# Buffers of the up projections' second pass and the modulation's transfers in a two-block transformer kernel

## The chip, the cores and the metric

The kernel runs as one program on one core of a Trainium2 chip. The metric is the time of one execution on the device in microseconds (us); several executions are timed and their median is given. A profiled execution, recorded by the hardware profiler, gives the trace from which all rows below are taken. TensorE (PE) multiplies, VectorE (DVE), ScalarE (ACT) and GpSimd (POOL) work on tiles in SBUF and PSUM, and SyncE (SP) issues most of the DMA transfers.

## The reference

Two transformer blocks on a sequence of 1024 tokens of width 1024, in float32. The first has a gated delta rule group and a latent attention group, the second a short convolution, stick-breaking attention and a modulation of six rows computed from a conditioning vector c. Both end in a feed-forward network of width 4096 with a squared ReLU. The change lies in the up projections of these two networks and in the modulation:

```python
# first block
h = rms_norm(x, ffn_pre_norm[l])
f = jnp.square(jax.nn.relu(h @ w_up[l])) @ w_down[l]
x = x + rms_norm(f, ffn_post_norm[l])
...
# second block
mod = c @ w_ada[l] + b_ada[l]
sh1, sc1, gt1, sh2, sc2, gt2 = jnp.split(mod, N_MOD, axis=-1)
...
h2 = modulate(rms_norm_2(x, g_pre_mlp[l]), sh2, sc2)
ff = jnp.square(jax.nn.relu(h2 @ w_mlp_in[l])) @ w_mlp_out[l]
x = x + gt2[:, None, :] * rms_norm_2(ff, g_post_mlp[l])
```

## The kernel before

The order of instructions on each engine is fixed when the program is built: a scheduler places them by its own estimate of times, under the waits that tiles and their buffers impose. Each engine then runs its instructions in that order, and SP issues its DMAs in its order. A named tile with `*n` in `TAGS` has n buffers used in turn; a new tile of that name waits until the readers and writers of the one n before are done.

All matrix products split each float32 operand into a high and a low part (`hi`, `lo`) and take three matmuls for one. The up projections, `ffn_up`, use a Strassen-like scheme in which 2x2 blocks need seven products. It is called twice by `up_stage`: in stage 1 with `w_up` (second pass from about 745 to 1010 us) and in stage 2 with `w_mlp_in_2` (second pass from about 2210 to 2470 us). A first pass makes two products per chunk of 256 columns and writes them to `fx_dr` in DRAM. The second pass runs over the 16 chunks c and makes the other five products, each 12 matmuls of 128x128 by 128x512, into PSUM tiles of which six may be in use (`mm_tile`).

For chunk c the second pass needs:

- the raw weights, 1 MB, from `load` (L1065). They go in turn into `w_raw` (even c) and into quarter 0 of a large tile, `hq` (odd c). The load of c+2 waits until the last reader of the raw weights of c is done.
- `fx` and `f00` from `load_x` (L1072), 256 KB each, both from `fx_dr`. The tile called `f00` here becomes `f11` in the loop (L1135) and is read by GpSimd at the end of the chunk; the trace calls it `f`.
- four sums and differences of quarters of the raw weights, from `weight_sums` (L1080) on VectorE; they go in turn into quarters 1 and 2 of `hq`. The fifth operand is a quarter of the raw weights themselves, called a22.
- for each of the five operands a split into high and low part (`parts`): two copies on ScalarE (L1093 and L1095) and a subtraction on VectorE (L1096). The split for a22 is the one whose L1096 reads `w_raw` or quarter 0 directly.

As products come, VectorE combines them (L1134, L1135, L1140, L1143, L1145, L1150, L1153), ScalarE applies ReLU and square (L1055, L1056), and GpSimd makes five more sums per chunk in tiles called `fs` (L1158) and stores them, 256 KB each (L1046). L1134 comes once per chunk.

In stage 1 the modulation runs beside this as `side`: it loads `w_ada_2` in slabs (L1275) into quarter 3 of `hq`, multiplies and adds them on VectorE (L1288, L1290), reduces each accumulated row on TensorE, copies it on ScalarE (L1246) and stores it with SP (L1247). The rest of the modulation runs in the same way beside the second block's convolution, with its own tiles `ada_raw`.

After the second pass, `ffn_down` loads weights (L1182) and the stored tiles (L1170).

Of the kernel before, what the change touches and what calls it, by code (L numbers as in the profile page):

```python
# [8 lines left out]
F32 = mybir.dt.float32  # L9
# [8 lines left out]
P = 128  # L18
# [15 lines left out]
TAGS = {  # L34
# [5 lines left out]
}  # L40
# [25 lines left out]
def tile_two_blocks(ctx: ExitStack, tc: tile.TileContext, I, out):  # L66
    nc = tc.nc
    PE, ACT, DVE, POOL, SP = nc.tensor, nc.scalar, nc.vector, nc.gpsimd, nc.sync
# [86 lines left out]
    mod_raw = scratch("mod_raw", (6, D))  # L155
# [94 lines left out]
    def col(r):  # L250
        return vec[:, r:r + 1]
# [790 lines left out]
    def ffn_up(hq, w_up, fl, fp, first, side):  # L1042
# [30 lines left out]

        def weight_sums(c):
            (a11, a21), (a12, a22) = ([raws[c][:, h, i] for i in range(2)] for h in range(2))
            t = fp.tile([P, 4, 4, P], F32, name="fws") if c == 0 else hq.tile(1 + c % 2, [P, 4, 4, P], F32)
            s1, s2, s3, s4 = (t[:, n] for n in range(4))
            for o, y, z, op in ((s1, a21, a22, ALU.add), (s2, s1, a11, ALU.subtract), (s3, a11, a21, ALU.subtract),
                                (s4, a12, s2, ALU.subtract)):
                DVE.tensor_tensor(out=o, in0=y, in1=z, op=op)  # L1080
            sums[c] = s2, s3, s1, a22, s4
# [16 lines left out]
        with tc.high_priority(offset=100):  # L1098
            for c in range(NC):
# [8 lines left out]
                for i, b in enumerate(("b11", "b21")):  # L1108
                    acc = product([t[:, 8 * (c % 2) + 4 * i:8 * (c % 2) + 4 * i + 4] for t in w], b)
# [8 lines left out]
        for c in range(NC):  # L1118
# [6 lines left out]
            x, f11 = xs.pop(c)  # L1125
# [29 lines left out]
            for i, y, z, o in ((0, f11, f22, ALU.add), (4, f11, f12, ALU.add), (6, f12, f22, ALU.subtract),  # L1155
                               (1, f21, f22, ALU.add), (5, f21, f11, ALU.subtract)):
                t = fp.tile([P, 512], F32, name="fs")
# [84 lines left out]
    def modulation_sum(i, acc, pool):  # L1242
        row = pool.tile([P, 512], F32, name="fs")[0:1, :]
        p = mm_tile()
        PE.matmul(p[0:1, :], ones[:, 0:1], acc, start=True, stop=True)
        ACT.copy(row, p[0:1, :])  # L1246
        SP.dma_start(mod_raw[i // 2:i // 2 + 1, (i % 2) * 512:(i % 2) * 512 + 512], row)  # L1247

    def modulation_columns(pool, m0, m1):

# [16 lines left out]
    def modulation(pool, m0, m1, new_raw, m):  # L1267

        n = 8 // m

        def load(j):
            if j < 2 * m1 * n:
                i, q = divmod(j, n)
                raw = new_raw()
                SP.dma_start(raw, I["w_ada_2"][0][m * P * q:m * P * q + m * P, 512 * i:512 * i + 512]  # L1275
                             .rearrange("(k p) n -> p k n", p=P))
                return raw

        raw, acc = load(2 * m0 * n), None
        yield  # L1280
        for i in range(2 * m0, 2 * m1):
            if acc is not None:
                modulation_sum(i - 1, acc, pool)
            acc = pool.tile([P, 512], F32, name="ada_acc")
            for k in range(8):
                r = raw[:, k % m, :]
                if k == 0:
                    DVE.tensor_scalar(acc, r, col(R_C), None, ALU.mult)  # L1288
                else:
                    DVE.scalar_tensor_tensor(out=acc, in0=r, scalar=col(R_C + k), in1=acc, op0=ALU.mult, op1=ALU.add)  # L1290
                if k % m == m - 1:
                    raw = load(n * i + k // m + 1)
                if k % 2:
                    yield
        modulation_sum(2 * m1 - 1, acc, pool)
        modulation_columns(pool, m0, m1)
# [264 lines left out]
    with ExitStack():  # L1561
        with banks(mm=6, tr=2):
            rows = {}

            def gains1(ep):
                for nm, v in (("gpost", "mix_post_norm"), ("grow", "ffn_pre_norm")):
                    rows[nm] = ep.tile([P, D], F32, name=nm)
                    bcast_row(rows[nm], I[v][0], D)

            def side1(fp, hq):  # L1570
                g = modulation(fp, 0, 2, lambda: hq.tile(3, [P, 4, 512], F32), 4)

                def step(c):
                    next(g, None)
                    if c == 15:
                        for _ in g:
                            pass

                return step

            mx1 = ExitStack()
            mxp = stage(mx1, "mx", 4, side="right")
            up_stage(1, I["w_out"][0], mix_dr, mxp, mx1, I["w_up"][0], lambda t, y, ep, put: epilogue(
                t, y, rows["gpost"], ep, I["x"][0], x_dr[0], lambda t, xt, xn, junk: norm_to_hT(
                    t, xt, xn, junk, None, None, row=rows["grow"], tmp_pool=ep, put=put), spare=False),
                "gpost grow xt*2 yg htt", gains1, side1)
            htx = ExitStack()
            edge(htx, "edge")
            h = new_hT(stage(htx, "hT", 1, side="right"))
            with sbuf("dp", 1, tags=TAGS["dp"]) as dp:  # L1590
                with sbuf("yf", 1, side="right") as yp, sbuf("ep", 1, side="right", tags="gpost xt*2 junk yg hmod*2") as ep:
                    y = yp.tile([P, NT, D], F32, name="y")
                    gf = ep.tile([P, D], F32, name="gpost")
                    bcast_row(gf, I["ffn_post_norm"][0], D)
                    first = ffn_down(I["w_down"][0], y, dp, lambda t: epilogue(
                        t, y[:, t, :], gf, ep, x_dr[0], x_dr[1],
                        lambda t, xt, xn, junk: norm_to_hT(t, xt, xn, junk, h[0], h[1], gain=amod[:, 0:8], bias=mod[:, 0:8], tmp_pool=ep)),
                        lambda i: w_cols(w_in2, (1024, 512)[i], 256))
            with sbuf("pb", 2) as pb, sbuf("pm", 1, tags="ada_acc*2 ada_raw*3 fs") as pm:
                side = modulation(pm, 2, 6, lambda: pm.tile([P, 2, 512], F32, name="ada_raw"), 2)  # L1600
                block2_conv_qkv(h, w_in2, pb, first, side)
                for _ in side:
                    pass
        with sbuf("so", 2) as so:
            with sbuf("pg", 2) as pg, sbuf("sp", 2, tags=TAGS["sp"]) as sp, banks(mm=2, sc=2, tr=2, po=2):
                for _ in stick_breaking(sp, so):
                    pass
                for _ in gates2(h, w_in2, pg):
                    pass
            htx.close()  # L1610
            late.enter_context(banks(mm=6, tr=2))
            mx2 = ExitStack()
            mxp2 = mx2.enter_context(sbuf("mx2", 4, side="right"))
            with sbuf("mg", 2) as mg:
                for half in range(2):
                    for _ in merge(half, mg):
                        pass
# [44 lines left out]
```

## Time and profile before

| | us |
|---|---|
| runs | 2832.03, 2825.65, 2827.81 |
| median of the runs | 2827.81 |
| profiled execution | 2816.81 |
| its span in the trace | 2815.0 |
| TensorE busy | 2648.2 (94%) |
| VectorE busy | 1920.3 (68%) |
| ScalarE busy | 1406.8 (50%) |
| GpSimd busy | 833.6 (30%) |

The busy shares are averages over stages with different limits. What a change in the second passes is worth has to be read from their stretches: how busy TensorE is there, what VectorE waits for, and in which order loads are issued and used.

### The profile page before, as it was taken

What the parts mean: (1) busy time and instruction counts of PE and PEld (TensorE: products, weight loads), DVE (VectorE), ACT (ScalarE), POOL (GpSimd) and SP (SyncE); (2) the same over time, 40 slices, a digit from 0 to 9 for tenths busy, and PEclk for the clock granted to TensorE, in tenths of its full rate; (3) what the DMA queues carried; (4) which work ended last, traced back from release to release, by engine and by line L of the source; (5) the groups of instructions that cost most, each with busy time, mean ns of one, the idle gap of its engine ahead of it and who ended that gap; (6) DMA issues with size and microseconds to landing.
All of it is one profiled execution on the core that took longest, in us unless ns stands there. A gap on an engine that the chain in (4) does not pass through costs nothing.

```text
span 2815.0 us, 39760 instructions
## 1 busy us (share of the span) xinstructions
PE 2648.2 (94%) x13801; PEld 2233.5 (79%) x13801; DVE 1920.3 (68%) x3518; ACT 1406.8 (50%) x2592; POOL 833.6 (30%) x840
## 2 busy tenths in 40 slices
PE   7999999999998889999999999999999998889996
PEld 7788889998777768777887788887798787668785
DVE  7678789858687765577755358686568575565666
ACT  5544666546665544354521246564267565543342
POOL 1242353200165562324100022111200165553413
PEclk9999999999999999999999999999999999999998
DMA  4286576446767677777664645334756666687785
GB/s 131 80 292 198 160 209 178 115 161 214 238 233 237 236 284 239 256 242 257 206 205 140 212 144 175 105 116 153 249 177 221 208 220 204 204 280 252 268 285 182
DMA packets 390207, 574.83 MB, mean 204 GB/s; under 512 B 39939, under 2 KB 224362, under 8 KB 390006
## 3 DMA queue, kind: packets, MB, share of 16 engines
q1 hardware_dynamic: 358774, 496.78, 55.1%
q0 software_dynamic: 12800, 41.95, 3.8%
q10 hardware_dynamic: 18432, 33.56, 3.2%
q8 instruction: 109, 1.79, 0.3%
q14 instruction: 92, 0.75, 0.1%
HBM read 417.21 MB, written 154.98 MB: 203 GB/s over the span
## 4 chain that ended last, share of the span: by engine, by line
PE 26%; DMA 17%; DVE 10%; POOL 6%; ACT 4%; issue 3%; SPq 1%; POOLq 0%; DVEq 0%; ACTq 0%
PE mm L173 22%; DMA dwr<-in_w_mlp_out 3%; DVE w_lo L179 3%; DMA w_raw<-in_w_down 3%; DMA f<-fx_dr 2%; POOL fs L1158 2%; POOL dwr L1186 2%; POOL w_raw L1186 1%; ACT w_hi L178 1%; DMA dwr<-in_w_down 1%; PE po L909 1%; DVE w_lo L209 1%; DMA w_raw<-in_w_mlp_out 1%; DMA w_raw<-in_w_mlp_in 1%; PE tr L901 1%
## 5 line engine op out<-in xcount | busy, mean ns | idle before, releaser
L173 PE MATMUL mm<-w_hi,df 128*128 128x512 f32 x1792 | 559.9, 393 | 11.8 <-DVE df L179 3.3
L173 PE MATMUL mm<-hq_t,w_hi 128*128 128x512 f32 x1280 | 410.4, 403 | 50.8 <-DVE fu L1150 23.0
L173 PEld LDWEIGHTS mm<-w_hi,df 128*128 128x128 f32 x1792 | 339.2, 190 | 86.5 <-DVE df L179 3.8
L173 PE MATMUL mm<-w_lo,df 128*128 128x512 f32 x896 | 353.2, 394 | 18.5 <-DVE w_lo L179 18.5
L173 PEld LDWEIGHTS mm<-hq_t,w_hi 128*128 128x128 f32 x1280 | 245.1, 194 | 117.3 <-issue 33.2
L173 PE MATMUL mm<-h_hi,w_hi 128*128 128x512 f32 x736 | 290.9, 395 | 0.0
L173 PE MATMUL mm<-h_lo,w_hi 128*128 128x512 f32 x736 | 289.4, 393 | 0.0
L173 PE MATMUL mm<-h_hi,w_lo 128*128 128x512 f32 x736 | 289.0, 393 | 0.0
L173 PE MATMUL mm<-hq_t,w_lo 128*128 128x512 f32 x640 | 253.5, 398 | 0.0
L209 DVE TENSOR_TENSOR w_lo<-w_raw,w_hi 128x1024 fp32r<-128x1024 f32 (+1 forms) x146 | 182.5, 1273 | 103.1 <-ACT w_hi L203 102.7
L203 ACT CAST w_hi<-w_raw 128x1024 fp32r<-128x1024 f32 (+1 forms) x146 | 147.0, 1049 | 166.9 <-PE mm L173 58.3
L173 PEld LDWEIGHTS mm<-w_lo,df 128*128 128x128 f32 x896 | 170.0, 190 | 59.0 <-DVE w_lo L179 24.1
L179 DVE TENSOR_TENSOR df<-dfr,df 128x1024 fp32r<-128x1024 f32 x112 | 157.9, 1422 | 77.4 <-ACT df L178 77.4
L1186 POOL TENSOR_TENSOR dwr<-dwr 128x1024 f32<-128x1024 f32 x40 | 101.2, 2530 | 320.0 <-DMA dwr<-in_w_mlp_out 183.1
L173 PE MATMUL mm<-w_hi,mixT 128*128 128x256 f32 x1024 | 183.7, 281 | 4.1 <-ACT w_hi L203 1.7
L179 DVE TENSOR_TENSOR w_lo<-dwr,w_hi 128x1024 fp32r<-128x1024 f32 x56 | 107.5, 1920 | 102.7 <-ACT w_hi L178 102.2
L178 ACT CAST df<-dfr 128x1024 fp32r<-128x1024 f32 x112 | 115.8, 1050 | 104.6 <-PE mm L173 62.9
L173 PEld LDWEIGHTS mm<-h_hi,w_hi 128*128 128x128 f32 x736 | 138.3, 188 | 34.0 <-issue 2.8
L173 PEld LDWEIGHTS mm<-w_hi,mixT 128*128 128x128 f32 x1024 | 156.7, 188 | 6.0 <-ACT w_hi L203 3.7
L1158 POOL TENSOR_TENSOR fs<-f,f 128x512 f32<-128x512 f32 x32 | 42.8, 1338 | 397.0 <-ACT f L1056 396.8
L173 PEld LDWEIGHTS mm<-h_hi,w_lo 128*128 128x128 f32 x736 | 138.3, 188 | 27.3
L173 PE MATMUL mm<-hq,w_hi 128*128 128x512 f32 x512 | 159.5, 392 | 0.0
(420 smaller groups left out, 6227.5 us busy)
## 6 DMA issues: line engine op xcount, KB each, us to landing
dfr<-fs SPq DMA_DIRECT2D x112, 512.0 KB
fs<-fs POOLq DMA_DIRECT2D x160, 256.0 KB, 5.3
w_raw<-in_w_in SPq DMA_DIRECT2D x32, 1024.0 KB
dwr<-in_w_down SPq DMA_DIRECT2D x48, 512.0 KB
w_raw<-in_w_down SPq DMA_DIRECT2D x48, 512.0 KB
dwr<-in_w_mlp_out SPq DMA_DIRECT2D x48, 512.0 KB
w_raw<-in_w_mlp_out SPq DMA_DIRECT2D x48, 512.0 KB
w_raw<-in_w_out SPq DMA_DIRECT2D x16, 1024.0 KB
```

The costliest lines, as they stand in the source:

```text
L173: PE.matmul(ps, l, r, start=first and n == 0, stop=final and n == last)
L178: ACT.copy(hi, src)
L179: DVE.tensor_tensor(out=lo, in0=src, in1=r32(hi), op=ALU.subtract)
L203: ins = ACT.copy(wh[:, step * i:step * i + step], raw[:, step * i:step * i + step])
L209: DVE.tensor_tensor(out=wl[:, c], in0=raw[:, c], in1=r32(wh[:, c]), op=ALU.subtract)
L901: PE.transpose(pt[:, 256 * j + P * i:256 * j + P * i + P], prob[i][:, ks], ident)
L909: PE.matmul(po[:, d:], vb if j else va, t[:, 256 * j:256 * j + 256 - d], start=n == 0 and m == 0, stop=n == len(groups) - 1 and m == 3)
L1158: POOL.tensor_tensor(out=t, in0=y, in1=z, op=o)
L1186: POOL.tensor_tensor(out=a, in0=a, in1=b, op=ALU.subtract if sub else ALU.add)
```

## The change

Five edits. The sums of all chunks but the first go into one quarter of `hq` (quarter 1) where two were used in turn. `fx` gets three buffers for two, `f00` four for two, `fs` four for seven. The modulation's slabs in stage 1 use quarters 2 and 3 in turn where quarter 3 alone was used, and each slab is loaded one slab earlier, in the convolution stage too. The modulation's row is stored by ScalarE's DMA queue where it was SP's. Line numbers from L1275 on are larger by two after the change.

```diff
--- before.py
+++ after.py
@@ -34,7 +34,7 @@
 TAGS = {
     "sp": "s_k*2 s_qh*2 s_ql*2 s_v s_b*4 s_r*2 pTh*2 pTl*2 po_lo*2",
     "gp": "g_kn0 g_knT0 g_dec0 g_AT0 g_X0 g_XT0 g_q0 g_v0 g_As0 g_Z0 g_Zl0 g_ke0 g_kn1 g_knT1 g_dec1 g_AT1 g_X1 g_XT1 g_q1 g_v1 g_As1 g_Z1 g_Zl1 g_ke1 g_sq*2 g_gate g_m",
-    "fp": "fws fx*2 f00*2 fu2*2 fu3*2 f11*2 fs*7 ada_acc",
+    "fp": "fws fx*3 f00*4 fu2*2 fu3*2 f11*2 fs*4 ada_acc",
     "dp": "dfr*2 df0*3 df1*3 dwr",
     "gq": "g_kn2 g_knT2 g_dec2 g_AT2 g_X2 g_XT2 g_q2 g_v2 g_As2 g_Z2 g_Zl2 g_ke2",
 }
@@ -1073,7 +1073,7 @@
 
         def weight_sums(c):
             (a11, a21), (a12, a22) = ([raws[c][:, h, i] for i in range(2)] for h in range(2))
-            t = fp.tile([P, 4, 4, P], F32, name="fws") if c == 0 else hq.tile(1 + c % 2, [P, 4, 4, P], F32)
+            t = fp.tile([P, 4, 4, P], F32, name="fws") if c == 0 else hq.tile(1, [P, 4, 4, P], F32)
             s1, s2, s3, s4 = (t[:, n] for n in range(4))
             for o, y, z, op in ((s1, a21, a22, ALU.add), (s2, s1, a11, ALU.subtract), (s3, a11, a21, ALU.subtract),
                                 (s4, a12, s2, ALU.subtract)):
@@ -1244,7 +1244,7 @@
         p = mm_tile()
         PE.matmul(p[0:1, :], ones[:, 0:1], acc, start=True, stop=True)
         ACT.copy(row, p[0:1, :])
-        SP.dma_start(mod_raw[i // 2:i // 2 + 1, (i % 2) * 512:(i % 2) * 512 + 512], row)
+        ACT.dma_start(mod_raw[i // 2:i // 2 + 1, (i % 2) * 512:(i % 2) * 512 + 512], row)
 
     def modulation_columns(pool, m0, m1):
 
@@ -1271,25 +1271,25 @@
         def load(j):
             if j < 2 * m1 * n:
                 i, q = divmod(j, n)
-                raw = new_raw()
+                raw = new_raw(j)
                 SP.dma_start(raw, I["w_ada_2"][0][m * P * q:m * P * q + m * P, 512 * i:512 * i + 512]
                              .rearrange("(k p) n -> p k n", p=P))
                 return raw
 
-        raw, acc = load(2 * m0 * n), None
+        ahead, acc = load(2 * m0 * n), None
         yield
         for i in range(2 * m0, 2 * m1):
             if acc is not None:
                 modulation_sum(i - 1, acc, pool)
             acc = pool.tile([P, 512], F32, name="ada_acc")
             for k in range(8):
+                if k % m == 0:
+                    raw, ahead = ahead, load(n * i + k // m + 1)
                 r = raw[:, k % m, :]
                 if k == 0:
                     DVE.tensor_scalar(acc, r, col(R_C), None, ALU.mult)
                 else:
                     DVE.scalar_tensor_tensor(out=acc, in0=r, scalar=col(R_C + k), in1=acc, op0=ALU.mult, op1=ALU.add)
-                if k % m == m - 1:
-                    raw = load(n * i + k // m + 1)
                 if k % 2:
                     yield
         modulation_sum(2 * m1 - 1, acc, pool)
@@ -1568,7 +1568,7 @@
                     bcast_row(rows[nm], I[v][0], D)
 
             def side1(fp, hq):
-                g = modulation(fp, 0, 2, lambda: hq.tile(3, [P, 4, 512], F32), 4)
+                g = modulation(fp, 0, 2, lambda j: hq.tile(2 + j % 2, [P, 4, 512], F32), 4)
 
                 def step(c):
                     next(g, None)
@@ -1597,7 +1597,7 @@
                         lambda t, xt, xn, junk: norm_to_hT(t, xt, xn, junk, h[0], h[1], gain=amod[:, 0:8], bias=mod[:, 0:8], tmp_pool=ep)),
                         lambda i: w_cols(w_in2, (1024, 512)[i], 256))
             with sbuf("pb", 2) as pb, sbuf("pm", 1, tags="ada_acc*2 ada_raw*3 fs") as pm:
-                side = modulation(pm, 2, 6, lambda: pm.tile([P, 2, 512], F32, name="ada_raw"), 2)
+                side = modulation(pm, 2, 6, lambda j: pm.tile([P, 2, 512], F32, name="ada_raw"), 2)
                 block2_conv_qkv(h, w_in2, pb, first, side)
                 for _ in side:
                     pass
```

The scheduler's order moves with the buffers. On SP, in the steady part of stage 2, before the change (numbers in names count tiles; `hq0` and `w_raw` are raw weights):

```order
L1065 DMA w_raw_24138<-in_w_mlp_in_2 128x8x256
L1072 DMA f00_24010<-fx_dr_98 128x512
L1072 DMA fx_24271<-fx_dr_98 128x512
L1065 DMA hq0_24269<-in_w_mlp_in_2 128x8x256
L1072 DMA f00_24141<-fx_dr_98 128x512
```

and after it:

```order
L1072 DMA f00_24141<-fx_dr_98 128x512
L1072 DMA fx_24271<-fx_dr_98 128x512
L1065 DMA w_raw_24138<-in_w_mlp_in_2 128x8x256
L1072 DMA f00_24272<-fx_dr_98 128x512
L1072 DMA fx_24402<-fx_dr_98 128x512
```

The f00 behind each raw load, and the fx ahead of it, now belong to later chunks (f00 by two, fx by one); that each raw load is preceded by an fx and followed by an f00 is unchanged.

On VectorE, from the L1096 of a22 that frees the buffer for `w_raw_24138` to the next L1135, before the change:

```order
L1096 TENSOR_TENSOR w_lo_22997<-w_raw_23876,tr_24097 128x512
L1140 TENSOR_TENSOR fu3_24058<-fu2_24035,mm_24041 128x512
L1096 TENSOR_TENSOR w_lo_23079<-hq1_24013,tr_24117 128x512
L1143 TENSOR_TENSOR f11_24077<-fu3_24058,mm_24060 128x512
L1145 TENSOR_TENSOR fu2_24035<-fu2_24035,mm_24060 128x512
L1096 TENSOR_TENSOR w_lo_23079<-hq2_24144,tr_24163 128x512
L1080 TENSOR_TENSOR hq1_24275<-w_raw_24138 128x512 x2
L1150 TENSOR_TENSOR fu3_24058<-fu3_24058,mm_24083 128x512
L1135 TENSOR_TENSOR f00_24010<-fx_24009,f00_24010 128x512
```

and after it:

```order
L1096 TENSOR_TENSOR w_lo_22997<-w_raw_23876,tr_24097 128x512
L1140 TENSOR_TENSOR fu3_24058<-fu2_24035,mm_24041 128x512
L1096 TENSOR_TENSOR w_lo_23079<-hq1_24013,tr_24117 128x512
L1080 TENSOR_TENSOR hq1_24144<-hq0_24007 128x512 x2
L1143 TENSOR_TENSOR f11_24077<-fu3_24058,mm_24060 128x512
L1145 TENSOR_TENSOR fu2_24035<-fu2_24035,mm_24060 128x512
L1080 TENSOR_TENSOR hq1_24144<-hq1_24144,hq0_24007 128x512
L1080 TENSOR_TENSOR hq1_24144<-hq0_24007,hq1_24144 128x512
L1150 TENSOR_TENSOR fu3_24058<-fu3_24058,mm_24083 128x512
L1135 TENSOR_TENSOR f00_24272<-fx_24271,f00_24272 128x512
```

The sums made here were those of the weights being loaded (`w_raw_24138`) and are now those of the weights loaded an iteration earlier (`hq0_24007`); L1135 reads the f00 that stands behind `w_raw_24138` on SP in both, `f00_24010` before and `f00_24272` after.

On SP at the end of the second pass of stage 2, before the change:

```order
L1072 DMA fx_24924<-fx_dr_98 128x512
L1182 DMA w_raw_25276<-in_w_mlp_out_2 128x2x512 x2
L1072 DMA f00_24796<-fx_dr_98 128x512
L1170 DMA dfr_25232<-fs2_101 128x1024
L1072 DMA f00_24925<-fx_dr_98 128x512
```

and after it:

```order
L1072 DMA f00_24796<-fx_dr_98 128x512
L1072 DMA fx_24924<-fx_dr_98 128x512
L1065 DMA hq0_24793<-in_w_mlp_in_2 128x8x256
L1072 DMA f00_24925<-fx_dr_98 128x512
L1182 DMA w_raw_25276<-in_w_mlp_out_2 128x2x512 x2
L1170 DMA dfr_25232<-fs2_101 128x1024
```

The last f00 loads stood between the first loads of the down projection and now stand ahead of them.

## Rows read from the trace of the kernel before

**Rows 1.** TensorE's busy time by stretches of stage 2: stretch, us, busy (x), PEclk, DMA share, GB/s

```profile
2240.00:2320.00 80.00, 80.00 (x354) 1.00 0.68 222
2320.00:2440.00 120.00, 103.94 (x432) 0.97 0.64 202
```

**Rows 2.** Timeline of TensorE, 2260 to 2264: start us, us, engine, line, operation

```profile
2260.22 0.62 PE L173 MATMUL mm<-hq_t,w_hi 128*128 128x512 f32 x2
...
2262.94 0.62 PE L173 MATMUL mm<-hq_t,w_hi 128*128 128x512 f32 x2
```

**Rows 3.** Instructions of L1134, stages 2 and 1: durations, first and last start

```profile
L1134 DVE TENSOR_TENSOR fu<-fx,mm x12: 673/679/681, 2283.0 to 2465.6; 128x512 f32<-128x512 f32 x12
...
L1134 DVE TENSOR_TENSOR fu<-fx,mm x12: 672/674/679, 824.0 to 1006.2; 128x512 f32<-128x512 f32 x12
```

**Rows 4.** Waits, 2190 to 2490: engine, line, waited for: us, times, longest

```profile
DVE hq L1080 <- DMA hq<-in_w_mlp_in: 33.8, 8, 6.4
DVE hq L1080 <- DMA w_raw<-in_w_mlp_in: 26.5, 5, 5.9
...
PE mm L173 <- DVE fu L1150: 15.6, 7, 3.0
```

**Rows 5.** Timeline of VectorE, 2331 to 2352; idle before in brackets

```profile
2333.15 0.69 DVE L1096 TENSOR_TENSOR w_lo<-w_raw,tr 128x512 fp32r<-128x512 f32 x1 [0.80 <-ACT tr L1095]
...
2342.74 1.29 DVE L1080 TENSOR_TENSOR hq<-w_raw 128x512 f32<-128x512 f32 x2 [5.92 <-DMA w_raw<-in_w_mlp_in]
...
2344.55 0.68 DVE L1135 TENSOR_TENSOR f<-fx,f 128x512 f32<-128x512 f32 x1
...
2350.05 0.69 DVE L1096 TENSOR_TENSOR w_lo<-hq,tr 128x512 fp32r<-128x512 f32 x1 [0.80 <-ACT tr L1095]
```

**Rows 6.** Timeline of SP's queue, 2330 to 2360

```profile
2333.86 0.38 SPq L1065 DMA_DIRECT2D w_raw<-in_w_mlp_in  x1
2336.17 0.32 SPq L1072 DMA_DIRECT2D f<-fx_dr  x1
...
2350.77 0.38 SPq L1065 DMA_DIRECT2D hq<-in_w_mlp_in  x1
```

**Rows 7.** Timeline of GpSimd, 2326 to 2355

```profile
2333.58 2.56 POOL L1158 TENSOR_TENSOR fs<-fu,f 128x512 f32<-128x512 f32 x2
```

**Rows 8.** Timeline of VectorE, end of stage 2's second pass

```profile
2314.49 0.68 DVE L1134 TENSOR_TENSOR fu<-fx,mm 128x512 f32<-128x512 f32 x1
...
2433.64 0.68 DVE L1134 TENSOR_TENSOR fu<-fx,mm 128x512 f32<-128x512 f32 x1
...
2445.92 1.16 DVE L1135 TENSOR_TENSOR f<-fx,f 128x512 f32<-128x512 f32 x1 [6.52 <-DMA f<-fx_dr]
```

**Rows 9.** Timeline of SP's queue, two loads of stage 1, one of stage 2

```profile
840.30 0.38 SPq L1065 DMA_DIRECT2D w_raw<-in_w_up  x1
...
893.88 0.38 SPq L1065 DMA_DIRECT2D hq<-in_w_up  x1
...
2435.84 0.95 SPq L1182 DMA_DIRECT2D w_raw<-in_w_mlp_out  x2
```

**Rows 10.** Timeline of VectorE, stage 1's second pass

```profile
851.41 0.69 DVE L1135 TENSOR_TENSOR f<-fx,f 128x512 f32<-128x512 f32 x1 [0.15 <-DMA f<-fx_dr]
...
899.18 1.29 DVE L1080 TENSOR_TENSOR hq<-hq 128x512 f32<-128x512 f32 x2 [1.86 <-DMA hq<-in_w_up]
...
984.62 1.04 DVE L1135 TENSOR_TENSOR f<-fx,f 128x512 f32<-128x512 f32 x1 [6.46 <-DMA f<-fx_dr]
```

**Rows 11.** Waits of SP's queue, 740 to 1035

```profile
SPq L1247 <- ACT fs L1246: 35.0, 3, 11.7
```

**Rows 12.** Waits of all engines, 740 to 1035

```profile
DVE ada_acc L1290 <- DMA hq<-in_w_ada: 8.2, 3, 4.8
```

**Rows 13.** Page, DMA issues: transfer, count, KB each, us to landing

```profile
fs<-fs POOLq DMA_DIRECT2D x160, 256.0 KB, 5.3
```

## The prediction

> **What bounds the kernel now.** I first read the engines' busy time by stretches, then the waits of the second passes, then the timelines of one iteration. The second pass of an up projection runs 16 iterations of five products, and a product is 12 matmuls. With nothing in the way twelve matmuls take 2.72 us, 2260.22 to 2262.94 [rows 2], so an iteration can't take less than 13.6 us of TensorE. From 2240 to 2320 us TensorE is indeed busy in all 80 of 80 us at full granted clock; from 2320 to 2440 it is busy in 103.9 of 120 at a mean granted clock of 0.97 [rows 1]. So the first iterations run on TensorE and the later ones on something slower. The step L1134, once per iteration, shows the pace: 12 of them from 2283.0 to 2465.6, or 16.6 us each, and 12 from 824.0 to 1006.2 in stage 1, again 16.6 [rows 3]. What is slow is VectorE: its weight sums L1080 wait for the raw weights in 13 iterations of stage 2, 33.8 and 26.5 us in all, about 4.6 each, and TensorE waits behind it for L1150, 15.6 us [rows 4].
>
> One iteration shows why this is a closed loop. SP issues the 1 MB of raw weights at 2333.86, as soon as L1096 of a22 at 2333.15 has read the old ones [rows 5, 6]. VectorE, in order, stands at L1080 from about 2336.8 until 2342.74, when they have landed [rows 5]. Then come two sums, L1150 and L1135 (2344.55), and after a chain with ScalarE the next a22 (2350.05) and with it the next raw load (2350.77) [rows 5, 6]. The period of 16.91 us is 8.88 (load) + 1.81 (to L1135) + 6.22 (L1135 to the next load). Whoever takes the wait at L1080 away gains only if nothing stands between load and L1135 for as long.
>
> **The change part by part.** *One buffer for sums.* The order on VectorE moves L1080 a whole iteration behind its load, since the sums of c+1 may only overwrite those of c once all five parts of c are made. That takes the wait of 60.3 us out, as the load is then 16 us old. The buffer adds no wait there: its readers stand ahead of its writer on the same engine.
>
> *Three buffers for x, four for f11.* They buy no distance between load and use. Before and after, L1135 stands about ten rows behind the a22 that releases the raw load, and takes the f00 whose load is queued directly behind that load; with four buffers it is only the f00 of a later iteration. No row of stage 2 shows L1135 waiting in the steady part, because the wait at L1080 ahead of it covered this. So the same loop closes through the other load: T = Lf + 6.22, with Lf the time from the issue of the raw weights to the use of the f00 behind them. The f00's issue still waits for GpSimd, which reads the old tile until 2336.14 [rows 7] before SP issues at 2336.17 [rows 6]; a ring of four doesn't free it sooner, as the tile that it frees is loaded for an iteration so much later. Break-even with the steady loop of before is Lf = 10.69.
>
> Lf has no row of its own in stage 2. Lower bound: f00 is queued behind the raw weights, which took 8.88 [rows 5, 6]. Upper bound: stage 1, where L1135 began at 851.41, having waited 0.15 for an f00 behind the weights of 840.30, 11.1 us [rows 9, 10]. Nearest is the end of stage 2, where the f00 already stands behind 1 MB of weights issued at 2435.84 and L1135 waits for it until 2445.92, that is 10.1 [rows 8, 9]. I take 10.1, so T = 16.3, with 15.1 and 17.3 at the ends. From 2314.49 to 2433.64 [rows 8] there are seven periods of 17.02: 7 x 0.7 = **-5** (-13 to +2). In the two before them, 31.5 us from 2283.0 [rows 3] to 2314.49, the wait was just building up; their floor is 27.2, and I credit **-3** (0 to -4).
>
> *The ends of both passes.* At the end, the f00 of the last two iterations stood behind weight loads of the down projection; now they are loaded two iterations earlier, ahead of those. The waits at 2445.92 (6.5 us) and in the last period go: from 2433.64 to 2465.6 there are two periods, 32.0 us, floor 27.2: **-4.7**. Stage 1 has the same wait, 6.46 at 984.62 [rows 10]: **-6** (bounded by 6.46 above and by 0, should the down projection's first loads, which follow on the same queue, only wait longer).
>
> *Stage 1, steady part.* Two kinds of iterations alternate here. Where the load is slow, f00 is already last (851.41), and nothing is won. Where it is fast (893.88 to 899.18, 5.3 us [rows 9, 10]), VectorE waited 1.86 and the loop was near TensorE's floor. **0** (-16 to +12, from the rivals below).
>
> *Modulation row on ScalarE's queue, weights two slabs ahead.* SP stood 35.0 us in three waits for the row [rows 11], 11.7 at most, but the next raw load also waited for a22, which came later in each; the issue costs ScalarE well under 1 us three times, in a stage where it idles with VectorE. The slabs' wait on VectorE, 8.2 us in three [rows 12], lies beside a raw wait of the same iteration. In the convolution stage, whose modulation uses the same code, TensorE doesn't wait for it. **0** (-3 to +2).
>
> *Four store tiles instead of seven.* GpSimd makes five per iteration; the fourth-last tile was stored about 5 us before it is needed, and a store takes 5.3 us to land [rows 13]. One operation per iteration may wait up to 2 us, the first of the next group, with over 5 us of idle behind it. **0** (0 to +20, a rival).
>
> Sum: -5 -3 -4.7 -6 = -18.7 on the profiled execution's 2816.8, so 2798.1. That execution was 11.0 us below the median of the runs, 2827.8; the forecast for the median is **2809**.
>
> **The rivals.** *Full release.* If the f00 lands soon enough (Lf up to 7.4), the loop falls below 13.6 and TensorE sets the pace. For it: the fast load of stage 1, 5.3 us; less idle time of VectorE shifts GpSimd's stores against the loads. Against it: GpSimd's work still hangs on L1135 through ScalarE, whose order puts the squares behind the wait, so that its stores meet the next raw load as before. Stage 2 then takes 11 x 13.6 = 149.6 instead of 182.6, -33; stage 1 about half of that, -16, since the modulation's operations share the loop: 2816.8 - 49 + 11 = **2779**. The Trainium skill, "DMA: Bandwidth & Descriptors", section "Anatomy of one DMA", gives a DMA (its fit is of GpSimd's path) 2.0 us plus its bytes at 436 GB/s; raw weights and f00 as one transfer of 1.31 MB would by this estimate land after 5.0 us, and the time would be that 2779. Rows 5, 6, 9 and 10 show 5.3 and 8.9 us for the weights alone, and the measurement decides here.
>
> *Nothing left.* Lf near 11: the steady loops lose what the ends gain, or the down projections, whose first loads are waited for anyway, take the ends' gain back. **2828**, 2822 to 2833.
>
> *Slower, by the store ring.* GpSimd holds the f00: its loads are issued when GpSimd's last reading is done. If with four store tiles GpSimd waits for landings within the group, not only ahead of it, each f00 is issued later. With 1.5 us of it on the nearest slow case, Lf is 11.6 and T 17.8: stage 2 has nine periods of 16.7 up to 2433.64, +9.7; stage 1 ten of 16.6, +12; the ends still give -10.7. **2839**. It decides from Lf of about 11.2, where the loops' loss passes the ends' gain. Against it: the 5 us of spacing above.
>
> **How the numbers follow.** Forecast (2797 to 2821) 0.48, full release 0.20, nothing left 0.15, slower 0.17. A measurement of this kernel can tell about 0.2% from no change, so faster is below 2822.2 and slower above 2833.5. Faster takes the forecast and the release, less 0.03 for their edges: 0.65; same 0.17; slower 0.18. The range leaves out half of the release's and half of the slower case's spread: 2777 to 2837.
>
> **What would show it.** In the second passes after: L1080 without a wait for a DMA; L1135 waiting for f00 about 3 to 5 us in most iterations, with TensorE still waiting behind VectorE for shorter times; L1134 about 16.3 us apart in stage 2 and 13.6 in its last two periods; no wait of 6.5 us at the ends. If L1135 doesn't wait and the steps are 13.6 apart, the release was right. If GpSimd waits for its stores inside a group and the f00's issue comes over 3 us behind the raw load, the slower rival is. The forecast is wrong where Lf is not near 10, since each us of it is worth about 18 us.

## The result

The changed kernel takes 2780.95 us (median of four runs, 2779.1 to 2783.0), the kernel before 2826.73 us (four runs): a ratio of 0.9837 with a 95% interval of 0.9818 to 0.9857. The forecast was 2809 us. The direction was right, but the gain is 46 us where 19 were forecast, and the time lies at the "full release" rival (2779), not at the likeliest case. One run further below, of the kernel with the buffer counts alone, took 3733.78 us at a granted clock of 0.653; it was in a slower state and stands in no median and no ratio here.

The profiled executions took 2779.1 and 2816.81 us. Where the difference lies is read from the first and last L1134 of both second passes. By instructions of L1134, the kernel before, stage 1 and stage 2 (the end of each row but for its shape is first to last start):

```profile
L1134 DVE TENSOR_TENSOR fu<-fx,mm x16: 672/674/686, 746.3 to 1006.2; 128x512 f32<-128x512 f32 x16
...
L1134 DVE TENSOR_TENSOR fu<-fx,mm x16: 673/679/686, 2214.1 to 2465.6; 128x512 f32<-128x512 f32 x16
```

and the changed kernel, with the middle of stage 2 in a row of its own:

```profile
L1134 DVE TENSOR_TENSOR fu<-fx,mm x16: 673/676/686, 744.3 to 994.6; 128x512 f32<-128x512 f32 x16
...
L1134 DVE TENSOR_TENSOR fu<-fx,mm x16: 673/678/689, 2206.7 to 2426.6; 128x512 f32<-128x512 f32 x16
...
L1134 DVE TENSOR_TENSOR fu<-fx,mm x8: 673/674/680, 2291.6 to 2386.3; 128x512 f32<-128x512 f32 x8
```

Stage 1's pass went from 259.9 to 250.3 us (-9.6), stage 2's from 251.5 to 219.9 (-31.6). Ahead of stage 1 it gained 2.0; between the passes 4.2 were lost again (1207.9 to 1212.1) and behind stage 2 another 1.3. That makes -37.7 of the span, 2815.0 to 2777.3. The medians lie 46 apart, since the profiled execution of before was faster than all four of its timed runs. In the middle of stage 2 the steps are (2386.3 - 2291.6) / 7 = 13.53 us, TensorE's floor. TensorE's busy time in one stretch, columns as in rows 1, in the kernel before:

```profile
2275.00:2395.00 120.00, 110.49 (x467) 0.97 0.66 212
```

and in the changed kernel:

```profile
2275.00:2395.00 120.00, 120.00 (x531) 1.00 0.74 245
```

It is busy in all 120 of 120 us at full granted clock, where it was 110.5 (and 103.9 of 120 in the slow stretch 2320 to 2440 [rows 1]).

The waits of VectorE in the changed kernel, 2170 to 2460 (us, times, longest), answer to rows 4:

```profile
DVE f L1135 <- DMA f<-fx_dr: 6.2, 4, 4.0
...
DVE hq L1080 <- DMA hq<-in_w_mlp_in: 1.7, 1, 1.7
```

The waits of the sums went from 60.3 us to 1.7, as forecast (that of the first chunk, in a tile of its own, is in neither number). But L1135 waits for f00 only 6.2 us in all, where 3 to 5 us in most chunks were forecast. One step of the changed kernel, SP's queue first:

```profile
2319.20 0.32 SPq L1072 DMA_DIRECT2D fx<-fx_dr  x1
2322.49 0.38 SPq L1065 DMA_DIRECT2D w_raw<-in_w_mlp_in  x1
...
2336.00 0.38 SPq L1065 DMA_DIRECT2D hq<-in_w_mlp_in  x1
```

and VectorE:

```profile
2318.49 0.67 DVE L1134 TENSOR_TENSOR fu<-fx,mm 128x512 f32<-128x512 f32 x1
2320.20 0.69 DVE L1096 TENSOR_TENSOR w_lo<-hq,tr 128x512 fp32r<-128x512 f32 x1 [1.04 <-ACT tr L1095]
2321.78 0.69 DVE L1096 TENSOR_TENSOR w_lo<-w_raw,tr 128x512 fp32r<-128x512 f32 x1 [0.88 <-ACT tr L1095]
...
2323.69 2.37 DVE L1080 TENSOR_TENSOR hq<-hq 128x512 f32<-128x512 f32 x2
...
2329.10 1.19 DVE L1135 TENSOR_TENSOR f<-fx,f 128x512 f32<-128x512 f32 x1
...
2342.90 0.88 DVE L1135 TENSOR_TENSOR f<-fx,f 128x512 f32<-128x512 f32 x1 [0.23 <-DMA f<-fx_dr]
```

The step is 13.51 us (2322.49 to 2336.00). L1135 at 2342.90 uses the f00 behind the raw weights of 2336.00, having waited 0.23 us for it: Lf is 6.90 us, where the prediction took 10.1 from bounds of 8.9 and 11.1.

All DMA queues together moved this in five and a half microseconds behind the issue of the raw weights, before (2333.86 to 2339.4):

```profile
DMA packets 990, 1.47 MB, mean 266 GB/s; under 512 B 49, under 2 KB 750, under 8 KB 990
```

and in the changed kernel (2322.49 to 2328.0):

```profile
DMA packets 1331, 1.84 MB, mean 333 GB/s; under 512 B 59, under 2 KB 1083, under 8 KB 1331
```

The raw weights move as 1024 packets of 1 KB, and in both traces no other packet here has between 512 B and 2 KB. So 750 - 49 = 701 of the 1024 had started in the kernel before, and 1083 - 59 = 1024, all, in the changed one. The load itself goes faster; the loop isn't just relieved of a wait. Why it goes faster is what the experiments had to find.

### The profile page after: what moved, and what is told of

It is laid out like the page before. It is cut to its first block, busy times and chain, and to the rows that moved or that the text cites. A ratio compares the mean times of both kernels' runs of the same rounds, so it can differ in the third digit from the quotient of the medians.

```text
span 2777.3 us, 39673 instructions
## 1 busy us (share of the span) xinstructions
PE 2637.3 (95%) x13801; PEld 2230.5 (80%) x13801; DVE 1946.2 (70%) x3518; ACT 1402.6 (51%) x2592; POOL 839.3 (30%) x840
## 4 chain that ended last, share of the span: by engine, by line
PE 31%; DMA 15%; DVE 12%; ACT 5%; POOL 4%; issue 4%; SPq 1%; ACTq 0%; POOLq 0%; DVEq 0%
PE mm L173 27%; DMA w_raw<-in_w_down 3%; DVE w_lo L179 3%; DMA dwr<-in_w_mlp_out 2%; DMA f<-fx_dr 2%; POOL w_raw L1186 2%; POOL dwr L1186 1%; ACT w_hi L178 1%; DMA dwr<-in_w_down 1%; DVE w_lo L209 1%; PE po L909 1%; DMA w_raw<-in_w_mlp_out 1%; PE tr L901 1%; POOL fs L1158 1%; ACT hmod L298 1%
## 5 line engine op out<-in xcount | busy, mean ns | idle before, releaser
L173 PE MATMUL mm<-hq_t,w_hi 128*128 128x512 f32 x1280 | 401.7, 397 | 26.8 <-ACT w_hi L1093 12.4
L179 DVE TENSOR_TENSOR df<-dfr,df 128x1024 fp32r<-128x1024 f32 x112 | 164.3, 1479 | 70.0 <-ACT df L178 69.8
L179 DVE TENSOR_TENSOR w_lo<-dwr,w_hi 128x1024 fp32r<-128x1024 f32 x56 | 109.2, 1949 | 111.0 <-ACT w_hi L178 110.5
L1158 POOL TENSOR_TENSOR fs<-f,f 128x512 f32<-128x512 f32 x32 | 48.8, 1524 | 433.4 <-ACT f L1056 433.4
L173 PEld LDWEIGHTS mm<-h_hi,w_hi 128*128 128x128 f32 x736 | 138.3, 188 | 33.9 <-issue 2.8
L178 ACT CAST df<-dfr 128x1024 fp32r<-128x1024 f32 x112 | 115.7, 1050 | 93.7 <-PE mm L173 57.8
L173 PEld LDWEIGHTS mm<-h_lo,w_hi 128*128 128x128 f32 x736 | 138.4, 188 | 26.5 <-issue 0.2
```

Source lines behind the costliest of these rows:

```text
L173: PE.matmul(ps, l, r, start=first and n == 0, stop=final and n == last)
L178: ACT.copy(hi, src)
L179: DVE.tensor_tensor(out=lo, in0=src, in1=r32(hi), op=ALU.subtract)
L1158: POOL.tensor_tensor(out=t, in0=y, in1=z, op=o)
```

## Experiments

**Which edit.** Four kernels, timed against the kernel before. The first has one edit:

```diff
-            t = fp.tile([P, 4, 4, P], F32, name="fws") if c == 0 else hq.tile(1 + c % 2, [P, 4, 4, P], F32)
+            t = fp.tile([P, 4, 4, P], F32, name="fws") if c == 0 else hq.tile(1, [P, 4, 4, P], F32)
```

> The kernel before with the one buffer for weight sums alone. Theory A (the wait of the sums for their raw weights closed the loop, and moving it suffices): TensorE sets the pace in stage 2, chunk steps of 13.5 us as in the changed kernel, the waits at the ends of the passes stay: about 2795 us. Theory B (the extra buffers for x and f11 are needed, else the loop closes on f00 at 16.3 us per chunk): 2815 us or more.

Measured: 2784.21 us, ratio 0.9837 (0.9802 to 0.9873), the whole gain within the intervals, and 11 us under the 2795 expected. Its TensorE in the same stretch of stage 2:

```profile
2275.00:2395.00 120.00, 120.00 (x532) 1.00 0.76 250
```

No stall and no low clock: with fx*2, f00*2 and fs*7 the loop is released as well. Theory A holds, theory B falls.

The second has the buffer counts alone:

```diff
-    "fp": "fws fx*2 f00*2 fu2*2 fu3*2 f11*2 fs*7 ada_acc",
+    "fp": "fws fx*3 f00*4 fu2*2 fu3*2 f11*2 fs*4 ada_acc",
```

> The kernel before with only fx*3, f00*4, fs*4. Theory A: the sums still wait for their own raw weights, steps stay near 17 us in stage 2, only the 6.5 us waits at the ends of the passes go: about 2815 us. Theory B: a good part of the gain, 2800 us or less.

Measured: 2817.23 us (median of nine runs), ratio 0.9954 (0.9932 to 0.9975). TensorE in that stretch:

```profile
2275.00:2395.00 120.00, 114.72 (x496) 0.99 0.66 219
```

Stalls remain, though fewer (114.7 us busy, before 110.5). The gain is half a per cent, as theory A had it, but not only from the ends of the passes. Its L1134 in stage 2:

```profile
L1134 DVE TENSOR_TENSOR fu<-fx,mm x16: 672/680/686, 2225.1 to 2459.3; 128x512 f32<-128x512 f32 x16
```

The pass took 234.2 us, 17 less than before, and stage 1's took 10 more (270.0). One of its steps, SP's queue:

```profile
2359.16 0.32 SPq L1072 DMA_DIRECT2D fx<-fx_dr  x1
2361.18 0.38 SPq L1065 DMA_DIRECT2D hq<-in_w_mlp_in  x1
```

VectorE there:

```profile
2368.16 1.29 DVE L1080 TENSOR_TENSOR hq<-hq 128x512 f32<-128x512 f32 x2 [4.03 <-DMA hq<-in_w_mlp_in]
```

The raw weights are usable after 7.0 us here, and after 6.6 to 8.2 in its eight slow steps from 2312 us on; before had 8.6 to 9.3 in its eight from 2299 us on. fx leaves 2.0 us ahead of them; this becomes the clue below.

The third has both of these edits, the fourth the ScalarE store of the row too; that is the changed kernel without the slabs two ahead (in the fourth, `load` of the modulation and its `new_raw` are those of before).

> One sums buffer and the new buffer counts, the modulation and its row store as before. Theory A: stage 2 as in the changed kernel, and stage 1 without what the modulation's edits give: 2781 to 2790 us. If the modulation's edits carry much (theory C), over 2795 us.

> The changed kernel with the modulation's slabs loaded one ahead into one quarter again; the row store stays on ScalarE. Theory A: within 0.3% of the changed kernel, about 2785 us. Theory C (the slabs two ahead carry stage 1's gain of 9.6 us): about 2791 us.

Measured: 2783.11 us, ratio 0.983 (0.9796 to 0.9865), and 2780.89 us, ratio 0.9829 (0.9786 to 0.9873). With the changed kernel at 0.9837 the three can't be told apart. On top of the single buffer of sums the other four edits bring nothing that these runs show, and theory C falls: stage 1's gain doesn't come from the slabs. In single profiled executions stage 1's pass took 255.5 us with the single buffer, 252.2 with the counts too, 247.4 with the row store too and 250.3 with all edits; but from its first L1134 to the first of stage 2 it is 1460.8, 1462.2, 1460.7 and 1462.4 us (before 1467.8), so what the later edits gain in this pass is lost again ahead of stage 2.

**Is the loop law right?** The prediction's step was T = Lf + 6.22, or TensorE's floor. If it is right, a slower f00 must bring the slow steps back. As a base, the f00 of stage 2 goes into two spare quarters (`hq.spare` is true in stage 2):

```diff
-            xs[c] = [fp.tile([P, 512], F32, name=nm) for nm in ("fx", "f00")]
+            xs[c] = [fp.tile([P, 512], F32, name=nm) for nm in (("fx",) if hq.spare else ("fx", "f00"))]
+            if hq.spare:
+                wide = hq.tile(2 + c % 2, [P, 4, 512], F32)
+                xs[c].append(wide[:, 0])
```

> The changed kernel with f00 of stage 2 in two spare quarters in turn, two buffers where it had four. It is the base for the next two. Theory A: two buffers are enough, steps of 13.5 us in stage 2, within 0.3% of the changed kernel (2781 us). If four buffers are needed, steps over 14 us.

Measured: 2791.44 us in one run, 0.4% over the changed kernel where 0.3% was the limit named. Steps in the middle of stage 2 are 13.5, so two buffers are enough there; the first chunks were slower, and TensorE waited 28.5 us for ScalarE (L178) at the start of the down projection. Onto this a load is put between raw weights and f00, of single elements, which take long for their few bytes (16 columns in the one, 32 in the other; the order of all engines stays):

```diff
+                if i and hq.spare and c > 3:
+                    for q in range(1):
+                        SP.dma_start(wide[:, 1, :16].rearrange("p (n two) -> p n two", two=1),
+                                     w_up[:P, 512:544].rearrange("p (n two) -> p n two", two=2)[:, :, :1])
```

> As wide0, but in stage 2 from chunk 4 on a slow extra load of 2048 single elements (8 KB, unused) stands on SP's queue between raw weights and f00; the order is that of wide0. The loop law of the prediction, T = max(13.5, Lf + 6.2), with Lf read from the trace: if the extra load makes Lf 9 to 11 us, steps of 15.2 to 17.2 and a time 15 to 45 us over wide0. If L1135's wait is not what closes the loop (theory F), steps stay at 13.5.

> As strided16 with twice as many elements (4096). By the loop law each further us of Lf is a further us of step: if the extra load costs 4 us per 2048 elements, Lf is about 15 and the steps 21 us. Theory F: steps stay at 13.5.

Measured: 2816.63 and 2827.69 us, one run each. SP's queue with 16 columns (below, L1141 is the operation that was L1135):

```profile
2338.61 0.38 SPq L1065 DMA_DIRECT2D hq<-in_w_mlp_in  x1
...
2354.32 0.38 SPq L1065 DMA_DIRECT2D w_raw<-in_w_mlp_in  x1
```

VectorE there:

```profile
2348.09 0.69 DVE L1141 TENSOR_TENSOR hq<-fx,hq 128x512 f32<-128x512 f32 x1 [2.79 <-DMA hq<-fx_dr]
```

and with 32 columns, SP's queue:

```profile
2330.44 0.38 SPq L1065 DMA_DIRECT2D w_raw<-in_w_mlp_in  x1
...
2347.36 0.38 SPq L1065 DMA_DIRECT2D hq<-in_w_mlp_in  x1
```

VectorE there:

```profile
2341.12 0.69 DVE L1141 TENSOR_TENSOR hq<-fx,hq 128x512 f32<-128x512 f32 x1 [4.04 <-issue]
```

With 16 columns Lf is 9.48 and the step 15.71, which leaves 6.23. With 32 Lf is 10.68, the step 16.92, which leaves 6.24 (the view names no releaser for this wait; a step later, with Lf 10.92, it names the DMA of f00). Lf varies, from 9.5 to 11.1 us with 16 columns and from 10.3 to 12.1 with 32, but in five steps of each from 2320 us on the step less Lf is 6.22 to 6.24. The law and its constant hold to two hundredths; theory F falls. (The second load cost less than I had guessed, so its steps were not 21.) At the 10.1 of the prediction the step would have been the 16.3 forecast. In this law only Lf was wrong.

**Why was the load slow before?** First, stores made small in the kernel before (`hq.extra` is true in stage 2):

```diff
-                left(c, i, t, POOL)
+                if hq.extra and c > 4:
+                    POOL.dma_start(fs_dr[i][:, 512 * c:512 * c + 64], t[:, 0:64])
+                else:
+                    left(c, i, t, POOL)
```

> The kernel before, except that in stage 2 from chunk 5 on each of GpSimd's five stores per chunk writes 64 of its 512 columns (the other columns of these arrays are left out, so the second block's feed-forward output is not the reference's). Order and waits are those of before. Theory D (the loads of raw weights took 8.9 us because the stores share the DMA engines with them): they land after 6 us or less, the loop of before closes at about 6 + 1.8 + 6.2 = 14 us or at TensorE's 13.5, and the time is 2790 us or less. Theory E (the slow load has another cause): steps stay near 17 us, 2815 us or more.

SP's queue:

```profile
2372.97 0.38 SPq L1065 DMA_DIRECT2D w_raw<-in_w_mlp_in  x1
...
2386.75 0.38 SPq L1065 DMA_DIRECT2D hq<-in_w_mlp_in  x1
```

VectorE there:

```profile
2378.15 1.78 DVE L1080 TENSOR_TENSOR hq<-w_raw 128x512 f32<-128x512 f32 x2 [2.21 <-DMA w_raw<-in_w_mlp_in]
```

L1080 starts 5.2 us behind the issue and the step is 13.8: with small stores even the old loop runs near TensorE's floor, as theory D has it. The whole, 2809.25 us in one run, missed the 2790: its steps came down only after 2342 us, and its second pass of stage 2 began some 9 us later than before's. Next, which stores (`i in (4, 6)` and `i in (1, 5, 0)` in the condition above, from chunk 4 on):

> The kernel before, except that in stage 2 from chunk 4 on the two stores that GpSimd issues just ahead of the next raw load (products 4 and 6) write 64 of 512 columns; the other columns are left out, so the output is not the reference's. Theory D1 (this pair, in flight with the x load when the raw load is issued, makes it slow): raw weights land after about 5.5 us, steps near 14 us. Theory D2 (the pair issued behind the raw load does it): they land after over 8 us, steps near 17.

> The kernel before, except that in stage 2 from chunk 4 on the other three stores of GpSimd (1, 5 and 0, issued behind the raw load) write 64 of 512 columns, the rest left out. Theory D1: raw weights still land after over 8 us, steps near 17. Theory D2: after about 5.5 us, steps near 14.

With the pair ahead of the raw load small (2797.99 us, one run), SP's queue:

```profile
2344.55 0.32 SPq L1072 DMA_DIRECT2D fx<-fx_dr  x1
2346.54 0.38 SPq L1065 DMA_DIRECT2D hq<-in_w_mlp_in  x1
```

VectorE there:

```profile
2351.85 1.63 DVE L1080 TENSOR_TENSOR hq<-hq 128x512 f32<-128x512 f32 x2 [2.35 <-DMA hq<-in_w_mlp_in]
```

GpSimd there:

```profile
2346.31 0.56 POOL L1160 DMA_DIRECT2D fs<-fs  x1
```

and with the three behind it small (2824.41 us, one run, inside the spread of before's own, 2814.5 to 2836.8 us in 13 runs), SP's queue:

```profile
2337.48 0.32 SPq L1072 DMA_DIRECT2D fx<-fx_dr  x1
2338.97 0.38 SPq L1065 DMA_DIRECT2D w_raw<-in_w_mlp_in  x1
```

VectorE there:

```profile
2348.21 1.29 DVE L1080 TENSOR_TENSOR hq<-w_raw 128x512 f32<-128x512 f32 x2 [6.28 <-DMA w_raw<-in_w_mlp_in]
```

5.3 us against 9.2 speaks for the pair stored just ahead of the raw load, theory D1. The two kernels differ in more than its size, though: in the first fx leaves 2.0 us ahead of the raw weights and in the second 1.5, and of the small pair only one store (L1160) is issued ahead, by 0.2 us, the other behind. And the changed kernel stores the whole pair at the same place as before. GpSimd in the kernel before:

```profile
2332.47 1.09 POOL L1046 DMA_DIRECT2D fs<-fs  x2
```

and in the changed kernel:

```profile
2321.23 1.10 POOL L1046 DMA_DIRECT2D fs<-fs  x2
```

These are 1.39 and 1.26 us ahead of the raw loads at 2333.86 [rows 6] and 2322.49. What differs is the fx load. In the kernel before SP's queue issued it here:

```profile
2332.37 0.32 SPq L1072 DMA_DIRECT2D fx<-fx_dr  x1
```

That is 0.1 us ahead of the pair and 1.5 ahead of the raw weights; in the changed kernel (2319.20) it is 2.0 ahead of the pair and 3.3 ahead of the raw weights. So one more kernel takes fx away from before and leaves all stores whole (`kept[0]` is the fx of chunk 4; `hq.extra` as above):

```diff
+            if hq.extra and c > 4:
+                xs[c] = [kept[0], fp.tile([P, 512], F32, name="f00")]
...
+                if i == 0 and hq.extra and c > 4:
+                    continue
```

> The kernel before, except that in stage 2 from chunk 5 on fx is not loaded: L1134 and L1135 read the fx of chunk 4 (so the output is not the reference's). All stores of GpSimd are whole. In the slow steps of before fx leaves 1.5 us ahead of the raw load and the pair of stores 1.4 us ahead. Theory G1 (the pair delays the raw weights only in company of the fx load): raw weights land after 6 us or less and the steps come to 14 us or less. Theory G2 (the pair is enough): landing after 8 us, steps of 16.5 us or more.

Measured: 2796.17 us in one run. SP's queue (below, L1086 is the sums' line):

```profile
2340.33 0.38 SPq L1065 DMA_DIRECT2D hq<-in_w_mlp_in  x1
...
2354.91 0.38 SPq L1065 DMA_DIRECT2D w_raw<-in_w_mlp_in  x1
```

VectorE there:

```profile
2346.35 1.29 DVE L1086 TENSOR_TENSOR hq<-hq 128x512 f32<-128x512 f32 x2 [3.06 <-DMA hq<-in_w_mlp_in]
```

The load is usable after 6.0 us and the step is 14.6; over the five loads from 2340 us on it is 6.0 to 6.7 us, and the steps between them are 14.5 to 15.2. That is a bit over what G1 named (6 and 14) and far from G2 (8 and 16.5). The pair alone doesn't make the load as slow as before. Nor does fx alone, as the trace of before shows in stage 1: the fast load of 893.88, usable at 899.18 [rows 9, 10], had fx just ahead and no store of GpSimd in the five microseconds ahead. SP's queue:

```profile
893.28 0.34 SPq L1072 DMA_DIRECT2D fx<-fx_dr  x1
```

The steps of all these traces, by what is issued ahead of the raw weights (from their issue to the start of the sums that wait for them):

| ahead of the raw weights | us | steps |
|---|---|---|
| one small store, fx 2.0 us | 5.2 to 5.5 | small pair, from 2317 us |
| fx 0.6 and 1.5 us, no store in 3.5 us | 5.3 and 5.2 | before, 893.88 and 2255.26 |
| fx 0.7 us, no store in 5 us | 6.2 to 7.6 | before, 2270.23, and the same step of the three kernels with small stores, ahead of these |
| the pair 1.3 us, no fx | 6.0 to 6.7 | no fx, from 2340 us |
| the pair 1.3 us, fx 2.0 us | 6.6 to 8.2 | buffer counts alone, from 2312 us |
| the pair 1.3 to 1.4 us, fx 1.2 to 1.5 us | 7.9 to 9.3 | before, from 2299 us; the three behind small, from 2304 us |

Either alone can cost about 1 to 2 us; the 8.6 to 9.3 of before come only with both close ahead. The packets of the traces say the same. In before's slow steps 96 to 112 of the 128 packets of fx (2 KB each) had not started when the raw weights were issued, and the last raw packet ended after 8.2 to 8.9 us. With the counts alone it was 11 to 48 packets and 6.2 to 7.9 us, and in the changed kernel's steps from 2295 us on none and 5.3 to 5.8 us, while nearly all of the pair's 0.5 MB was still to move in each of them. (The ScalarE store behind the raw load also moved, from 3.1 to 5.5 us after its issue; but it stands at 3.1 in the loads of 5.3 and 6.0 us above too, so it isn't what makes 9.) In the two slowed kernels above, with steps of 15.7 us and more, fx too leaves 3.1 us ahead, so the f00's delay was the added load's, and the spacing comes with the order, not with the pace. (Without fx one operation on VectorE also changed places with its neighbours; the wait that is read here stands as before.)

**A version to beat both?** Stage 1's steps are still 16.7 us on average, with VectorE working on the modulation in between. So TensorE takes these products over:

```diff
+            if m == 4:
...
+                    for k in range(8):
...
+                        PE.matmul(p[0:1, :], col(R_C + k), raw[:, k % m, :], start=k == 0, stop=k == 7)
...
+                continue
```

> The changed kernel with the modulation of stage 1 made by TensorE (eight matmuls of one column by a slab of 512 per row, accumulated in PSUM) in place of 32 multiply-adds of VectorE and a matmul with ones. VectorE loses about 35 us of work in stage 1, TensorE gains 28 x 0.59 = 17 us. If VectorE's bursts of these operations are what keeps stage 1's steps at 16.7 us on average, stage 1 shortens by 25 us less 17, and the time is 2765 to 2775 us; if something else holds stage 1, the added matmuls cost and it is 2785 to 2795.

Measured: 2776.86 us (2773.05 to 2782.28), ratio 0.9824 (0.9796 to 0.9852), just beside the changed kernel and just over the 2765 to 2775 expected. Instructions of L1134 in stage 1:

```profile
L1134 DVE TENSOR_TENSOR fu<-fx,mm x16: 673/687/689, 749.0 to 990.7; 128x512 f32<-128x512 f32 x16
```

TensorE's group of the new products, 740 to 1000 us (busy, mean ns, idle before):

```profile
L1290 PE MATMUL mm<-hq,vec 128*1 128x512 f32 x64 | 28.1, 592 | 0.0
```

The pass takes 241.7 us for 250.3, but starts 4.7 us later. Seven of its steps are at 13.60, and three, with eight products of the modulation each, at 20.0 to 20.9: about 7 us for eight, 0.9 each and not the 0.59 of one record that I had counted with. The 64 records belong to 32 matmuls, two each, and 28.1 us for 32 is 0.88. VectorE's bursts did hold stage 1, but TensorE pays most of it back. It is not shown to beat the changed kernel.

## Why the prediction was wrong in its size

- **What bounded the kernel.** Right. The loop of raw load, sums, L1135 and a22 held stage 2, and taking the sums out of it alone gave the gain (2784 us with that edit).
- **One buffer for sums.** Right: the wait of 60.3 us became 1.7, and the single buffer added none that these rows show.
- **The new law, T = Lf + 6.22.** Right, with 6.22 to 6.24 in ten steps of the two slowed kernels.
- **Lf = 10.1.** This is the step that failed. It measured 6.9 where L1135 waited for it in the step above, and 7.5 at most in the steady steps (2349.47), so the steps came to TensorE's floor instead of 16.3 and stage 2 gave 31.6 us instead of 12.7. My lower bound, 8.88, was the load time of before, taken as if a load's duration went with its bytes and with GpSimd's stores alone; the 5.3 us of rows 9 and 10, which I called the fast load, already lay under it. And all three cases that the 10.1 and its bounds came from had fx 1.2 to 1.5 us ahead. I had checked that the stores keep their place against the raw load, and they do. I hadn't looked at the other transfer there: in the new order one more L1096 stands between L1134, which frees fx, and a22, which frees the raw weights (2318.49, 2320.20, 2321.78 above). Both wait for ScalarE, so fx leaves 3.3 us ahead instead of 1.5, and the bunch of fx, pair and raw weights is gone. The order is fixed when the program is built, so this could have been read before any run; the excerpt that I gave of it begins at the L1096 of a22, one L1134 and one L1096 too late.
- **The release rival** was right in mechanism for stage 2 (Lf under 7.4, TensorE sets the pace), but I gave it 0.20. Of its reason, the shifted stores, nothing is left; it was fx that shifted. That its 2779 lies within 2 us of the measured 2780.95 is luck in part: it took -49 from both stages, where the profiled execution shows -31.6 and -9.6, and added 11 us for the median, which lies only 2 above the profiled execution. The fit of the page "DMA: Bandwidth & Descriptors" of the Trainium skill, section "Anatomy of one DMA", gave an estimate of 5.0 us for raw weights and f00. L1135 used the f00 at 6.6 and 6.9 us, nearer to this than to my 10.1; but the fit has no place for what is issued just ahead, and that was worth over 3 us here.
- **Slow loads still come.** In one early step of the changed kernel three stores were issued just ahead of a raw load. SP's queue:

```profile
2265.51 0.38 SPq L1065 DMA_DIRECT2D w_raw<-in_w_mlp_in  x1
```

GpSimd there:

```profile
2264.80 1.63 POOL L1046 DMA_DIRECT2D fs<-fs  x3
```

VectorE there:

```profile
2276.28 0.69 DVE L1135 TENSOR_TENSOR f<-fx,f 128x512 f32<-128x512 f32 x1 [4.01 <-DMA f<-fx_dr]
```

  Lf was 10.8 there, as large as I feared, and L1135 waited 4.0 us; but it happened once in this trace, and the following steps were near the floor. The spacing isn't the whole, either: in the kernel with the first two edits and in that without the slabs two ahead, single steps (raw weights at 2350.00 and 2292.91) had Lf of 9.3 and 9.0 with the changed kernel's spacing.
- **The ends.** In time their part can't be singled out: the buffer counts alone gave half a per cent, but with other changes in both passes, and on top of the single buffer of sums nothing that shows (2784.2 and 2783.1 us). In the traces the last two steps of stage 2 took 32.0 us before, 28.8 with the single buffer and 26.6 with all edits, so the -4.7 came there.
- **Stage 1.** -6 was forecast, at the end of its pass, and 0 in the steady part. -9.6 came in the profiled execution, of which 4.2 were lost again before stage 2, and not where I put it: the last two steps took 33.5 us before and 33.9 after, so the gain lies in the 13 steps ahead. This forecast was wrong in its place, and no run shows what keeps the last two steps long.
- **Modulation and row store** at 0, **store ring** at 0: right as far as shown; without the slabs the time is 2780.89.
- **Left open.** Why fx and the pair together cost the raw load 3 to 4 us, when it took 6.0 to 6.7 us with the pair alone and 5.2 to 7.6 with fx alone, no run shows. The bytes alone don't explain it: all queues together moved less in the slow case (1.47 MB in 5.5 us against 1.84). The trace doesn't tell which of the 16 engines carried which packet.

## What to carry to other kernels

A load's time in the old trace belongs to the old order: before it is used as a bound for the new one, list every transfer issued in the microseconds ahead of it, from all queues, and look in the new order for what frees each of them. Where a wait closes a loop, write the loop as a sum and ask of each term whether it would be the same in the new order; here one of three was not. And where a chunk loop has a floor set by TensorE, a latency under the slack costs nothing and one above it costs its excess on every chunk, so that a small error in the latency can decide between no loss and a loss in every step.

## What the runs showed of the hardware

The same 1 MB load was used 5.2 to 5.5 us after its issue with one small store and a 256 KB load 2.0 us ahead, 6.0 to 6.7 with a whole pair of 256 KB stores and no other load, 6.6 to 8.2 with that load 2.0 us ahead and the pair, and 7.9 to 9.3 with the load and the pair all issued within 1.5 us ahead of it. With a load of 2048 single elements, 8 KB, ahead of it the f00 was used 9.5 to 11.1 us after the issue of the raw weights, with one of 4096 after 10.3 to 12.1, where the kernel without them had 7.1 at most in its steady steps. A float32 matmul of one column by 512 is recorded twice, with 592 ns each, and costs TensorE about 0.9 us in a row of eight.
